# Forgetting attention: the keys' cumulative sums and the causal mask enter the logits by matmuls in PSUM instead of by VectorE

## The chip, the cores and the metric

One of the eight cores of a Trainium2 chip runs the whole kernel. The metric is device time in microseconds, the median of repeated runs. The engines are TensorE (PE, with its weight loads PEld), VectorE (DVE), ScalarE (ACT), GpSimd (POOL) and the DMA queue that SyncE (SP) issues. Everything is float32 in and out; products of full accuracy are made of three TensorE passes over a high and a low half (`hi*hi`, `hi*lo`, `lo*hi`), each half in the rounded type fp32r.

## The reference, cut to what matters

The layer normalises x (512 tokens, width 1024), projects it by one wide matrix, runs four mixers side by side (a chunked spatial gate, a top-k attention, a gated convolution, a forgetting attention), gates and merges them, and projects back. Only the forgetting attention changes:

```python
cum = jnp.cumsum(jax.nn.log_sigmoid((f_logit + b_f).astype(jnp.float32)), axis=1)
cum_k = jnp.transpose(cum, (0, 2, 1))
...
logits = jnp.einsum('bqhd,bshd->bhqs', qb, kh).astype(jnp.float32) * (FOX_HEAD_DIM ** -0.5)
logits = logits + jnp.transpose(cq, (0, 2, 1))[..., None] - cum_k[:, :, None, :]
logits = jnp.where((key_pos[None, :] <= pos_q[:, None])[None, None], logits, -jnp.inf)
p = jax.nn.softmax(logits, axis=-1).astype(vh.dtype)
o = jnp.einsum('bhqs,bshd->bqhd', p, vh)
```

So each logit gets the query's cumulative sum (one number per row and head), minus the key's cumulative sum (one number per column and head), and a mask above the diagonal.

## The kernel before, in words

Weights stream in by 256 columns (`load_w`), ScalarE and VectorE or GpSimd split them into halves (`split`, `unit`), and `proj_fm` makes a 128-feature by 512-token product of 24 matmuls of 512 columns (L119, L120, L124). Between such products the kernel calls `point()`, which advances two generators by one step: `topk_steps` (first `cumulate`, then `scores_topk`) and `attn_steps` (`attention`). A scheduler that simulates the engines then orders the instructions of each engine, so a step's work can land some matmuls earlier or later than it is written.

`scores_topk` is VectorE's longest job: for three blocks of queries it forms scores (matmuls `dots`, L458 and L459, the second with only 64 rows), and then takes 16 rounds of MAX8 and MATCH_REPLACE8 over each block (`sc1`, `sc2`, `sc3`).

`attention` runs 16 jobs, one per head h and query block i, each over n = 128(i+1) keys; `fox` is the forgetting attention. A job makes three logit matmuls into a PSUM bank `lg` (`mm3`, L88 to L90; two at i = 0, L502 and L505). Then VectorE adds the query's sum `cq` and a tile `nb[h]` of the keys' sums (L509), adds the mask to the diagonal block (L511; at i = 0 also the second half of the bank, L515), and takes the row maximum (L517). ScalarE exponentiates with the maximum as bias (L519), VectorE inverts the sum (L521), ScalarE scales (L522). Three jobs later (`lag`) TensorE transposes the result (`pt_ps`, L533), which is split into halves again, and after four jobs of a head `values` makes the products `po` with the values. The `nb[h]` tile comes from `neg_cum` (L434): the row h of the four cumulative sums is picked and split (`rh` on ScalarE, `rl` on VectorE, L84) and two matmuls with 4 rows and 512 columns (`nb_ps`, L439 and L440) spread it over 128 partitions.

Three pools matter. `tmp` gives out 512-column SBUF tiles in turn (9 of them). PSUM has 4 banks `mm` for the projections and 4 banks `at` for everything else, `lg`, `pt_ps`, `po`, `dots` among them. SBUF-to-SBUF work of GpSimd (`wl`, L81, 2.4 us each in this stage) runs beside VectorE's.

Of the kernel before, what the change touches and what calls it, by code (L numbers as in the profile page):

```python
# [8 lines left out]
F32 = mybir.dt.float32  # L9
F32R = mybir.dt.float32r  # L10
AF = mybir.ActivationFunctionType
ALU = mybir.AluOpType
# [11 lines left out]
NH = 4  # L24
# [9 lines left out]
def hybrid_kernel(ctx: ExitStack, tc, x, norm_g, w_in, gm_ln_g, gm_ln_b, gm_w_s, gm_b_s,  # L34
# [26 lines left out]
        return big(name + "h"), big(name + "l")  # L61

    def tmp(name, dtype=F32, cols=S):
        return sb.tile([P, cols], dtype, tag="tmp", name=name, bufs=9)

    def small(name, cols=1, bufs=4):
        return sb.tile([P, cols], F32, tag=name, name=name, bufs=bufs)
# [1 line left out]
    def psum(name):  # L69
        return at.tile([P, S], F32, tag="at", name=name)  # L70
# [117 lines left out]
    def load_dv(i):  # L188
# [11 lines left out]
    load_x(2)  # L200
    load_x(3)

    ident = const.tile([P, P], F32, name="ident")
    make_identity(nc, ident)
    negh = const.tile([P, 8], F32, name="negh")
    nc.vector.memset(negh, -0.5)
    causal = const.tile([P, P], F32, name="causal")
    nc.gpsimd.memset(causal, 0.0)
    nc.gpsimd.affine_select(out=causal, in_=causal, compare_op=ALU.is_ge, fill=-BIG, base=0,
                            pattern=[[-1, P]], channel_multiplier=1)  # L210
    up = const.tile([P, S], F32R, name="up")
    upf = tmp("upf")
    nc.gpsimd.memset(upf, 1.0)
# [119 lines left out]
    for u in range(2):  # L333
        ps = proj_fm(unit(rawq, u))
        qf, qs = tmp("qf"), tmp("qs")
        nc.scalar.activation(qf, ps, AF.Copy)
        nc.sync.dma_start(qs[0:64], qf[64:128])
        nc.sync.dma_start(qs[64:128], qf[0:64])

        even, odd, low = (kq[(2 + 3 * u + i) // 4][:, (2 + 3 * u + i) % 4, :] for i in range(3))  # L340
        for dst, own, other in ((even, slice(0, 64), slice(64, 128)), (odd, slice(64, 128), slice(0, 64))):
            nc.scalar.activation(dst[own], qf[own], AF.Copy)
            nc.scalar.activation(dst[other], qs[other], AF.Copy)
            nc.vector.tensor_tensor(low[own], qf[own], dst[own].bitcast(F32), op=ALU.subtract)
        qis += [(even, low), (odd, low)]
        if u == 0:
            sp = psum("sp")
            rp = psum("rp")
            nc.tensor.transpose(rp[:, 0:13], rows, ident[0:13, 0:13])
            for t in range(NT):  # L350
                nc.tensor.transpose(sp[:, 8 * t:8 * t + 8], wf[64:72, t * P:(t + 1) * P],
                                    ident[64:72, 64:72])
            prm = const.tile([P, 45], F32, name="prm")
            nc.vector.tensor_copy(prm[:, 0:32], sp[:, 0:32])
            nc.vector.tensor_copy(prm[:, 32:45], rp[:, 0:13])
            wif = prm[:, 0:32].rearrange("p (t c) -> p t c", c=8)
            kvg = prm[:, 44:45]

            sq = tmp("sq")
            nc.scalar.activation(sq, ps_c, AF.Square)  # L360
            sqh, sql = (tmp("sq" + s, F32R) for s in "hl")
            split(sqh, sql, sq)
            ms = psum("ms")
            for t in range(NT):
                ts_ = slice(t * P, (t + 1) * P)
                nc.tensor.matmul(ms[:, 2 * t:2 * t + 2], sqh[:, ts_], up[:, P:P + 2],
                                 start=True, stop=False)
                nc.tensor.matmul(ms[:, 2 * t:2 * t + 2], sql[:, ts_], up[:, P:P + 2],
                                 start=False, stop=True)
            rc = small("rc", 2 * NT, 1)  # L370
            rsqrt(rc, ms[:, 0:2 * NT], 1.0 / P, 2 * NT)
        else:

            dg = sb.tile([P, NT, P], F32, tag="tmp", name="dg", bufs=9)
            nc.vector.tensor_tensor(dg, ident[:, None, :].to_broadcast([P, NT, P]),
                                    rc[:, 0::2, None].to_broadcast([P, NT, P]), op=ALU.mult)
            dgh, dgl = (tmp("dg" + s, F32R) for s in "hl")
            split(dgh, dgl, dg.rearrange("p t c -> p (t c)"))
            rb_ = psum("rb")
            nc.tensor.matmul(rb_, up[:, P:2 * P], dgh, start=True, stop=False)  # L380
            nc.tensor.matmul(rb_, up[:, P:2 * P], dgl, start=False, stop=True)
            cn = tmp("cn")
            nc.scalar.activation(cn, ps_c, AF.Copy)
            nc.vector.tensor_tensor(cn, rb_, cn, op=ALU.mult)
            cth = const.tile([P, S], F32R, name="cth")
            ctl = const.tile([P, S], F32R, name="ctl")
            split(cth, ctl, cn, kvg)


    def flat16(tl):  # L390
        return tl.rearrange("p t h -> p (t h)")
# [15 lines left out]
    nc.vector.tensor_tensor(z_, z_, e_, op=ALU.mult)  # L407
    nc.vector.tensor_tensor(l_, l_, z_, op=ALU.add)
    nc.vector.scalar_tensor_tensor(ls, f16, 0.0, l_, op0=ALU.min, op1=ALU.subtract)
    lsh = const.tile([P, NT, NH], F32R, name="lsh")  # L410
    lsl = const.tile([P, NT, NH], F32R, name="lsl")
    split(flat16(lsh), flat16(lsl), ls)


    cq = const.tile([P, NT, NH], F32, name="cq")
    nb = {}

    def cumulate():
        ps = psum("cum")
        for j in range(NT):  # L420
            for n, part in enumerate((lsh, lsl)):
                nc.tensor.matmul(ps[0:NH, j * P:], part[:, j, :], up[:, 0:S - j * P],
                                 start=(j == 0 and n == 0), stop=(j == NT - 1 and n == 1))
        cum = tmp("cum")[0:NH, :]
        nc.scalar.activation(cum, ps[0:NH, :], AF.Copy, scale=-1.0)
        yield
        ps = psum("cq")
        for t in range(NT):
            nc.tensor.transpose(ps[:, NH * t:NH * t + NH], cum[:, t * P:(t + 1) * P],
                                ident[0:NH, 0:NH])  # L430
        nc.scalar.activation(flat16(cq), ps[:, 0:16], AF.Copy, scale=-1.0)
        nb["rows"] = cum

    def neg_cum(h):  # L434

        rh, rl = (tmp("r" + x, F32R)[0:NH, :] for x in "hl")
        split(rh, rl, nb["rows"], ident[0:NH, h:h + 1])
        ps = psum("nb_ps")
        nc.tensor.matmul(ps, up[0:NH, P:2 * P], rh, start=True, stop=False)  # L439
        nc.tensor.matmul(ps, up[0:NH, P:2 * P], rl, start=False, stop=True)  # L440
        nb[h] = tmp("nb")
        nc.scalar.activation(nb[h], ps, AF.Copy)


    msk = {0: causal}
# [43 lines left out]
    def attention(qks, vh, vl, o, fox, lag=3):  # L489
# [3 lines left out]
        def logits(h, i):  # L493
            qh, ql = qks[h][:, 0, :], qks[h][:, 1, :]
            kh, kl = key_parts(qks[h])
            n = (i + 1) * P
            qs = slice(i * P, n)
            ps = psum("lg")
            l = tmp("l")
            if i == 0:  # L500

                nc.tensor.matmul(ps[:, 0:2 * P], qh[:, qs],  # L502
                                 qks[h][:, 2:4, :].rearrange("p a c -> p (a c)")[:, 0:2 * P],
                                 start=True, stop=False)
                nc.tensor.matmul(ps[:, 0:P], ql[:, qs], kh[:, 0, :], start=False, stop=True)  # L505
            else:
                mm3(ps[:, :n], qh[:, qs], ql[:, qs], kh[:, 0:i + 1, :], kl[:, 0:i + 1, :], True, True)
            if fox:
                nc.vector.scalar_tensor_tensor(l[:, :n], ps[:, :n], cq[:, i, h:h + 1],  # L509
                                               nb[h][:, :n], op0=ALU.add, op1=ALU.add)  # L510
                nc.vector.tensor_tensor(l[:, qs], l[:, qs], causal, op=ALU.add)  # L511
            else:
                nc.vector.tensor_tensor(l[:, :n], ps[:, :n], msk[i], op=ALU.add)
            if i == 0:
                nc.vector.tensor_tensor(l[:, :n], ps[:, P:2 * P], l[:, :n], op=ALU.add)  # L515
            nm = small("nm")
            nc.vector.tensor_reduce(nm, l[:, :n], axis=AX.X, op=ALU.max, negate=True)  # L517
            se = small("se")
            nc.scalar.activation(l[:, :n], l[:, :n], AF.Exp, bias=nm, accum_out=se)  # L519
            ri = small("ri")  # L520
            nc.vector.reciprocal(ri, se)  # L521
            nc.scalar.activation(l[:, :n], l[:, :n], AF.Copy, scale=ri)  # L522
            ls[h, i] = l
# [39 lines left out]
    def fox_qk(hp):  # L563
        rq = load_w(D_Q + hp * 256)
        rk = load_w(D_K + hp * 256)
        for s in range(2):
            h = 2 * hp + s
            neg_cum(h)
            qk = qk_tile("qk")
            ps = proj_fm(unit(rq, s))  # L570
            split(qk[:, 0, :], qk[:, 1, :], ps, scale)
# [10 lines left out]
    gps = at.tile([P, NH, P], F32, tag="at", name="gps")  # L582
    for g in range(NH):
        nc.tensor.transpose(gps[:, g, :], gw[:, g * P:(g + 1) * P], ident)
    gwt = sb.tile([P, NH, P], F32, tag="tmp", name="gwt", bufs=9)
    nc.vector.tensor_copy(gwt, gps)
    nc.gpsimd.affine_select(out=gwt, in_=gwt, compare_op=ALU.is_ge, fill=0.0, base=0,
                            pattern=[[0, NH], [1, P]], channel_multiplier=-1)
# [27 lines left out]
    def mixed(cp):  # L616
        ru = load_w(A_U + cp * 256)
        for s in range(2):
            g = 2 * cp + s
            ps = proj_fm(unit(ru, s))  # L620
            gs = slice(g * P, (g + 1) * P)
            t1 = sb.tile([P, NT, P], F32, tag="tmp", name="t1", bufs=9)
            for c2 in range(0, NT, 2):
                mx = at.tile([P, 2, 2, P], F32, tag="at", name="mx")
                for c in range(2):
# [244 lines left out]
```

## Time and profile before

| | |
|---|---|
| three runs | 710.55 us median (708.91 to 711.37) |
| the profiled execution: its own time | 711.89 us |
| its span, first to last instruction | 710.2 us |
| PE busy | 693.9 us (98%), 3139 matmuls |
| DVE busy | 364.5 us (51%), of 110 to 170 us all of it |
| ACT busy | 275.1 us (39%) |
| the forgetting attention's jobs | first logits at 127.5 us, L509 of the last job at 212.2 us |

TensorE's busy time is drawn from modelled ends: in a stream of 512-column matmuls each is shown 0.39 us long, though the next starts 0.227 us after it. What a matmul costs is therefore read from one start to the next. The profile's share of DVE is a mean: it is idle most of the second half and has no gap in the stretch of the top-k rounds.

### The profile page before, as it was taken

Reading aid. Unit: us, or ns where it says so; the run is one execution under the profiler, and the core shown is the slowest. Engines: PE = TensorE matmul, PEld = TensorE weight load, DVE = VectorE, ACT = ScalarE, POOL = GpSimd, SP = SyncE. Lnnn points to the kernel's source line nnn. Section 1 sums busy time; section 2 is a strip of 40 time slices with the busy share of each in tenths; the row PEclk is TensorE's granted clock in tenths of the full one; section 3 lists DMA queues with packets and bytes.
Section 4 is the critical chain, followed back from the end, with each engine's and each line's share of the span. In section 5 each row is a group of like instructions: output and inputs, shape, how many; then the busy total and the mean of one; then the engine's idle time right before and its main releaser. Section 6 shows DMA issues by size and latency. Waiting matters only on the chain.

```text
span 710.2 us, 8000 instructions
## 1 busy us (share of the span) xinstructions
PE 693.9 (98%) x3139; PEld 566.4 (80%) x3139; DVE 364.5 (51%) x638; ACT 275.1 (39%) x439; POOL 169.9 (24%) x110
## 2 busy tenths in 40 slices
PE   7999999988999999999999999999999999999996
PEld 4878767766888888888888888888888888888885
DVE  5825699999953664634233343323522334343454
ACT  4616354354444556433322242223322223333233
POOL 1000487341333323203000021222211132111101
PEclk9999999999999999999999999999999999999999
DMA  6715031312112111242322331322313313133233
GB/s 237 219 64 153 4 118 59 112 59 69 60 60 90 60 60 60 61 147 73 105 83 96 118 114 65 119 77 102 120 60 118 117 61 119 60 118 119 62 117 119
DMA packets 56817, 68.05 MB, mean 96 GB/s; under 512 B 3582, under 2 KB 45067, under 8 KB 56780
## 3 DMA queue, kind: packets, MB, share of 16 engines
q1 hardware_dynamic: 55900, 65.46, 28.3%
q0 software_dynamic: 304, 1.05, 0.4%
q10 hardware_dynamic: 576, 1.05, 0.4%
q8 instruction: 24, 0.39, 0.2%
q14 instruction: 13, 0.11, 0.0%
HBM read 64.80 MB, written 2.10 MB: 94 GB/s over the span
## 4 chain that ended last, share of the span: by engine, by line
PE 85%; DVE 11%; DMA 2%; issue 1%; ACT 0%; SPq 0%; POOLq 0%; POOL 0%; DVEq 0%
PE ps_fm L119 18%; PE ps_fm L120 18%; PE ps_fm L124 18%; PE pb L744 4%; PE pb L745 4%; PE pb L747 4%; DVE sc L474 3%; DVE m L473 2%; PE ps_o L144 2%; PE ps_o L146 2%; PE ps_o L145 2%; DVE sc L466 1%; PE pt_ps L533 1%; PE ps_dv L144 1%; DVE l L511 1%
## 5 line engine op out<-in xcount | busy, mean ns | idle before, releaser
L119 PE MATMUL ps_fm<-hh,wh 128*128 128x512 f32 (+1 forms) x640 | 251.3, 393 | 0.0
L120 PE MATMUL ps_fm<-hl,wh 128*128 128x512 f32 (+1 forms) x640 | 250.0, 391 | 0.0
L124 PE MATMUL ps_fm<-hh,wl 128*128 128x512 f32 (+1 forms) x640 | 162.5, 391 | 0.0
L119 PEld LDWEIGHTS ps_fm<-hh,wh 128*128 128x128 f32 (+1 forms) x640 | 120.1, 188 | 26.0 <-issue 0.9
L120 PEld LDWEIGHTS ps_fm<-hl,wh 128*128 128x128 f32 (+1 forms) x640 | 120.0, 187 | 24.9 <-issue 0.2
L124 PEld LDWEIGHTS ps_fm<-hh,wl 128*128 128x128 f32 (+1 forms) x640 | 119.0, 187 | 25.0 <-issue 0.2
L80 ACT ACTIVATE wh<-raw 128x1024 fp32r<-128x1024 f32 x78 | 82.3, 1056 | 114.1 <-PE ps_fm L120 85.0
L81 DVE TENSOR_TENSOR wl<-raw,wh 128x1024 fp32r<-128x1024 f32 x50 | 61.0, 1222 | 78.4 <-PE ps_fm L124 67.1
L81 POOL TENSOR_TENSOR wl<-raw,wh 128x1024 fp32r<-128x1024 f32 x28 | 69.1, 2474 | 111.9 <-PE ps_fm L124 49.2
L753 POOL TENSOR_TENSOR acc<-acc,sg 128x512 f32<-128x512 f32 x24 | 41.8, 1742 | 155.9 <-DVE sg L752 155.9
L744 PE MATMUL pb<-yh,wh 128*128 128x512 f32 x128 | 49.8, 389 | 0.0
L745 PE MATMUL pb<-yl,wh 128*128 128x512 f32 x128 | 49.8, 389 | 0.0
L81 DVE TENSOR_TENSOR wl<-rawb,wh 128x1024 fp32r<-128x1024 f32 x16 | 19.6, 1225 | 51.3 <-PE ps_fm L124 36.8
L80 ACT ACTIVATE wh<-rawb 128x1024 fp32r<-128x1024 f32 x16 | 16.9, 1057 | 50.6 <-PE ps_fm L120 50.6
L752 DVE TENSOR_TENSOR sg<-pb,sg 128x512 f32<-128x512 f32 x24 | 16.6, 692 | 36.3 <-PE pb L747 36.3
L747 PE MATMUL pb<-yh,wl 128*128 128x512 f32 x128 | 34.2, 389 | 0.0
L519 ACT ACTIVATE l<-l,nm 128x128 f32<-128x128 f32 (+3 forms) x32 | 17.9, 560 | 28.5 <-DVE nm L517 28.5
L771 ACT ACTIVATE sg<-ps_fm 128x512 f32<-128x512 f32 x32 | 19.2, 600 | 24.4 <-PE ps_fm L124 24.4
L747 PEld LDWEIGHTS pb<-yh,wl 128*128 128x128 f32 x128 | 24.0, 188 | 5.0
L744 PEld LDWEIGHTS pb<-yh,wh 128*128 128x128 f32 x128 | 24.0, 188 | 5.0
L745 PEld LDWEIGHTS pb<-yl,wh 128*128 128x128 f32 x128 | 24.0, 188 | 5.0
L145 PE MATMUL ps_o<-wl,mh 128*128 128x512 f32 (+1 forms) x72 | 26.2, 366 | 0.0
(242 smaller groups left out, 913.9 us busy)
## 6 DMA issues: line engine op xcount, KB each, us to landing
raw<-in_w_in_dram SPq DMA_DIRECT2D x39, 1024.0 KB, 4.9
rawb<-in_w_branch_dram SPq DMA_DIRECT2D x8, 1024.0 KB, 4.9
rawt<-in_w_out_dram SPq DMA_DIRECT2D x4, 1024.0 KB, 4.9
xt<-in_x_dram SPq DMA_DIRECT2D x4, 512.0 KB, 8.3
rawt<-in_w_in_dram SPq DMA_DIRECT2D x4, 512.0 KB, 8.4
rawt<-in_w_in_dram SPq DMA_DIRECT2D x2, 1024.0 KB, 5.7
xr<-in_x_dram SPq DMA_DIRECT2D x2, 1024.0 KB, 4.9
out_dram<-o SPq DMA_DIRECT2D x4, 256.0 KB, 2.1
```

What stands on the lines that cost most here:

```text
L80: nc.scalar.activation(hi, src, AF.Copy)
L81: eng.tensor_tensor(lo, src, hi.bitcast(F32), op=ALU.subtract)
L119: nc.tensor.matmul(ps[:m], wh[:, k, :], hh[:, k, :], start=(k == 0), stop=False)
L120: nc.tensor.matmul(ps[:m], wh[:, k, :], hl[:, k, :], start=False, stop=False)
L124: nc.tensor.matmul(ps[:m], wl[:, k, :], hh[:, k, :], start=False, stop=(k == NK - 1))
L144: nc.tensor.matmul(ps, ah, wh, start=(k == 0), stop=False)
L145: nc.tensor.matmul(ps, ah, wl, start=False, stop=False)
L474: nc.vector.match_replace(out=scs[i], in_to_replace=m8, in_values=scs[i], imm_value=TAKEN)
L744: nc.tensor.matmul(pb, bh[:, k, cs_], yh[:, k, :], start=(k == 0), stop=False)
L745: nc.tensor.matmul(pb, bh[:, k, cs_], yl[:, k, :], start=False, stop=False)
L747: nc.tensor.matmul(pb, bl[:, k, cs_], yh[:, k, :], start=False, stop=(k == NH - 1))
L753: nc.gpsimd.tensor_tensor(acc, acc, sg, op=ALU.add)
```

## The change

The keys' sums are no longer spread over partitions by `neg_cum`. `cumulate` now makes the four cumulative sums twice, in rows 0 to 3 and 32 to 35 of a 36-row tile; ScalarE rounds them to fp32r (`cums`), and VectorE leaves the rounding rest in rows 32 to 35. A 36 by 4 tile `pick` holds ones at rows h and 32+h. In each job of the forgetting attention two matmuls follow the three logit products in the same bank: the identity times the causal mask on the diagonal block (128 columns, L515 of the new file), and `pick`'s column h, spread over 128 output rows, times `cums` (36 rows, n columns, L517). VectorE takes the row maximum from PSUM, and one 1-column instruction (`nb`, L523) folds the query's sum into the bias; ScalarE exponentiates from PSUM. At i = 0 the products are three of 128 columns instead of one of 256 and one of 128. The identity and the mask are kept as fp32r, made by VectorE casts from `tmp` tiles, and `tmp` has 8 tiles instead of 9. The other attention keeps its old path.

```diff
-        return sb.tile([P, cols], dtype, tag="tmp", name=name, bufs=9)
+        return sb.tile([P, cols], dtype, tag="tmp", name=name, bufs=8)
...
-    ident = const.tile([P, P], F32, name="ident")
-    make_identity(nc, ident)
+    identf = tmp("identf", cols=P)
+    make_identity(nc, identf)
+    identr = const.tile([P, P], F32R, name="ident")
+    nc.vector.tensor_copy(identr, identf)
+    ident = identr.bitcast(F32)
+
+    pick = const.tile([36, NH], F32R, name="pick")
+    nc.vector.tensor_copy(pick, identf[0:36, 0:NH])
+    nc.vector.tensor_copy(pick[32:36, :], identf[32:36, 32:36])
...
     def cumulate():
-        ps = psum("cum")
+        l36 = tmp("l36")[:, 0:144].rearrange("p (t c) -> p t c", c=36)
...
+        cum = tmp("cum")[0:36, :]
+        nc.scalar.activation(cum, ps, AF.Copy, scale=-1.0)
+        nc.scalar.activation(cums, cum, AF.Copy)
+        nc.vector.tensor_tensor(cums[32:36, :], cum[32:36, :], cums[32:36, :].bitcast(F32),
+                                op=ALU.subtract)
...
-    def neg_cum(h):
-
-        rh, rl = (tmp("r" + x, F32R)[0:NH, :] for x in "hl")
-        split(rh, rl, nb["rows"], ident[0:NH, h:h + 1])
-        ps = psum("nb_ps")
-        nc.tensor.matmul(ps, up[0:NH, P:2 * P], rh, start=True, stop=False)
-        nc.tensor.matmul(ps, up[0:NH, P:2 * P], rl, start=False, stop=True)
-        nb[h] = tmp("nb")
-        nc.scalar.activation(nb[h], ps, AF.Copy)
...
+            if fox:
+
+                ks_ = slice(0, i + 1)
+                nc.tensor.matmul(ps[:, :n], qh[:, qs], kh[:, ks_, :], start=True, stop=False,
+                                 skip_group_check=True)
+                nc.tensor.matmul(ps[:, :n], qh[:, qs], kl[:, ks_, :], start=False, stop=False,
+                                 skip_group_check=True)
+                nc.tensor.matmul(ps[:, :n], ql[:, qs], kh[:, ks_, :], start=False, stop=False,
+                                 skip_group_check=True)
+                nc.tensor.matmul(ps[:, qs], identr, causalr, start=False, stop=False,
+                                 skip_group_check=True)
+                nc.tensor.matmul(ps[:, :n], pick[:, h:h + 1].to_broadcast([36, P]), cums[:, :n],
+                                 start=False, stop=True, skip_group_check=True)
+
+                nc.vector.tensor_reduce(nm, ps[:, :n], axis=AX.X, op=ALU.max, negate=True)
+                c = cq[:, i, h:h + 1]
+                nb = small("nb")
+                nc.vector.tensor_scalar(nb, nm, c, c, op0=ALU.subtract, op1=ALU.add)
+                src, bias = ps[:, :n], nb
...
-            if fox:
-                nc.vector.scalar_tensor_tensor(l[:, :n], ps[:, :n], cq[:, i, h:h + 1],
-                                               nb[h][:, :n], op0=ALU.add, op1=ALU.add)
-                nc.vector.tensor_tensor(l[:, qs], l[:, qs], causal, op=ALU.add)
...
-            nc.scalar.activation(l[:, :n], l[:, :n], AF.Exp, bias=nm, accum_out=se)
+            nc.scalar.activation(l[:, :n], src, AF.Exp, bias=bias, accum_out=se)
...
-            neg_cum(h)
```

Because `cumulate` has become longer, the scheduler places the first score products elsewhere. On TensorE before, the third product of the spatial gate (`ps_va_747`) is interrupted for them, with 2 of its 24 matmuls and the whole fourth product (`ps_va_814`) still to come:

```order
L144 MATMUL ps_va_747<-wh_601,hh_58 128x512
L429 MATMUL cq_655<-ident_96,cum_653 128x4 x4
L458 MATMUL dots_662<-kq_407 128x256
L459 MATMUL dots_662<-kq_407,kq_408 128x256
...
L145 MATMUL ps_va_747<-wl_602,hh_58 128x512
L146 MATMUL ps_va_747<-wh_601,hl_59 128x512
L144 MATMUL ps_va_814<-wh_587,hh_58 128x512
```

On TensorE now, they come behind all four products and behind 12 matmuls of the first query projection (`ps_fm_898`; new line numbers):

```order
L119 MATMUL ps_fm_898<-hh_58,wh_894 128x512
L120 MATMUL ps_fm_898<-hl_59,wh_894 128x512
L445 MATMUL cq_669<-ident_101,cum_665 128x4 x4
L463 MATMUL dots_676<-kq_414 128x256
L464 MATMUL dots_676<-kq_414,kq_415 128x256
L463 MATMUL dots_682<-kq_414 128x256
L464 MATMUL dots_682<-kq_414,kq_415 128x256
L463 MATMUL dots_688<-kq_414,kq_415 128x256
```

The first scores thus moved behind 2 + 24 + 12 = 38 more matmuls of 512 columns. The job itself, on VectorE: before, around the third and fourth job of the first head (`l_1163`, `l_1196`), among the top-k rounds:

```order
L509 SCALAR_TENSOR_TENSOR l_1163<-lg_1162,cq_570,nb_886 128x384
L474 MATCH_REPLACE sc1_661<-m8_1566,sc1_661 128x256
L473 MAX m8_1159<-sc3_795 128x8
L515 TENSOR_TENSOR l_1095<-lg_1094,l_1095 128x128
L474 MATCH_REPLACE sc2_728<-m8_1156,sc2_728 128x384
L511 TENSOR_TENSOR l_1163<-l_1163,causal_103 128x128
L473 MAX m8_1675<-sc1_661 128x8
L474 MATCH_REPLACE sc3_795<-m8_1159,sc3_795 128x512
L517 TENSOR_REDUCE nm_1101<-l_1095 128x1
```

Now, around the first two jobs of that head (`lg_1081`, `lg_1116`):

```order
L520 TENSOR_REDUCE nm_1083<-lg_1081 128x1
L478 MAX m8_1030<-sc2_742 128x8
L478 MAX m8_952<-sc3_809 128x8
L479 MATCH_REPLACE sc1_675<-m8_1185,sc1_675 128x256
L523 TENSOR_SCALAR nb_1090<-nm_1083,cq_573 128x1
L479 MATCH_REPLACE sc2_742<-m8_1030,sc2_742 128x384
L479 MATCH_REPLACE sc3_809<-m8_952,sc3_809 128x512
L478 MAX m8_1269<-sc1_675 128x8
L542 RECIPROCAL ri_1094<-se_1092 128x1
```

Of a job's wide VectorE instructions one is left, and two of one column (L523, L542) stand beside it, with top-k rounds between them as before.

## Rows read from the trace of the kernel before

**Rows 1.** The page: busy us, share of the span, instructions.

```profile
PE 693.9 (98%) x3139; PEld 566.4 (80%) x3139; DVE 364.5 (51%) x638; ACT 275.1 (39%) x439; POOL 169.9 (24%) x110
```

**Rows 2.** The chain of waits in order of time: start, us, what.

```profile
310.08 1.81 PE ps_fm L124 x8
```

**Rows 3.** Stages: us, busy us and count of PE, PEld, DVE, ACT, POOL; clock, DMA.

```profile
160.00:169.00 9.00, 6.07 (x25) 3.86 (x24) 9.00 (x27) 3.72 (x9) 1.31 (x1) 1.00 0.03 9
169.00:173.00 4.00, 4.00 (x18) 3.77 (x17) 4.00 (x13) 2.59 (x8) 1.07 (x1) 0.57 0.46 144
```

**Rows 4.** What PE waited for: us in total, times, longest us.

```profile
PE nb_ps L440 <- DVE rl L84: 1.5, 1, 1.5
PE po L89 <- DVE ptl L81: 1.5, 1, 1.5
PE pt_ps L533 <- DVE l L515: 0.9, 1, 0.9
PE pt_ps L533 <- ACT l L522: 0.7, 2, 0.4
PE gp L263 <- DMA g<-in_norm_g_dram: 0.3, 1, 0.3
```

**Rows 5.** PE in order of time at 147 us: start, us, what.

```profile
147.29 0.33 PE L533 MATMUL pt_ps<-ident,l 128*128 128x128 f32 x1 [0.29 <-ACT l L522]
147.55 0.50 PE L439 MATMUL nb_ps<-rh,up 4*128 4x512 f32 x1
149.54 0.50 PE L440 MATMUL nb_ps<-rl,up 4*128 4x512 f32 x1 [1.49 <-DVE rl L84]
```

**Rows 6.** PE in order of time: a 4-row matmul among 128-row ones.

```profile
109.85 0.39 PE L120 MATMUL ps_fm<-hl,wh 128*128 128x512 f32 x1
110.17 0.50 PE L439 MATMUL nb_ps<-rh,up 4*128 4x512 f32 x1
110.60 0.50 PE L119 MATMUL ps_fm<-hh,wh 128*128 128x512 f32 x1
110.94 0.39 PE L120 MATMUL ps_fm<-hl,wh 128*128 128x512 f32 x1
```

**Rows 7.** PE in order of time: a 64-row matmul among 128-row ones.

```profile
102.37 0.39 PE L458 MATMUL dots<-kq 128*128 128x512 f32 x1
102.69 0.49 PE L459 MATMUL dots<-kq 64*128 64x512 f32 x1
103.11 0.50 PE L119 MATMUL ps_fm<-hh,wh 128*128 128x512 f32 x1
103.45 0.40 PE L120 MATMUL ps_fm<-hl,wh 128*128 128x512 f32 x1
```

**Rows 8.** PE in order of time: 256-column and 128-column matmuls.

```profile
155.75 0.28 PE L90 MATMUL lg<-qk 128*128 128x256 f32 x1
155.87 0.49 PE L533 MATMUL pt_ps<-ident,l 128*128 128x128 f32 x3
156.11 0.95 PE L124 MATMUL ps_fm<-hh,wl 128*128 128x512 f32 x3
```

**Rows 9.** DVE's busy us (count) from 127.4 to 168.7 us, of L509 alone.

```profile
127.40:168.70 41.30, 3.44 (x7) 1.00 0.20 67
```

**Rows 10.** The same of L511 alone.

```profile
127.40:168.70 41.30, 7.55 (x7) 1.00 0.20 67
```

**Rows 11.** PE, PEld and DVE of tile rl alone, 80 to 168.7 us.

```profile
80.00:168.70 88.70, 1.98 (x4) 0.72 (x4) 3.09 (x4) 1.00 0.22 72
```

**Rows 12.** DVE and POOL in order of time at 135.8 us.

```profile
135.82 2.40 POOL L81 TENSOR_TENSOR wl<-raw,wh 128x1024 fp32r<-128x1024 f32 x1 [4.61 <-PE ps_fm L124]
135.89 2.47 DVE L511 TENSOR_TENSOR l<-l,causal 128x128 f32<-128x128 f32 x1
```

**Rows 13.** Lines L511 and L521: count: min/median/max ns, first and last start.

```profile
L511 DVE TENSOR_TENSOR l<-l,causal x16: 264/277/2471, 135.9 to 213.5; 128x128 f32<-128x128 f32 x16
L521 DVE RECIPROCAL ri<-se x32: 131/154/166, 146.7 to 290.6; 128x1 f32<-128x1 f32 x32
```

More of the change, by code (lines that the diff above doesn't have):

```diff
@@ L201, in hybrid_kernel @@
     load_x(3)
-    ident = const.tile([P, P], F32, name="ident")
-    make_identity(nc, ident)
+    identf = tmp("identf", cols=P)
[6 more added lines that the diff above has]
+    nc.vector.tensor_copy(pick[32:36, :], identf[32:36, 32:36])
     negh = const.tile([P, 8], F32, name="negh")
     nc.vector.memset(negh, -0.5)
-    causal = const.tile([P, P], F32, name="causal")
-    nc.gpsimd.memset(causal, 0.0)
-    nc.gpsimd.affine_select(out=causal, in_=causal, compare_op=ALU.is_ge, fill=-BIG, base=0,
+    causalf = tmp("causalf", cols=P)
+    nc.gpsimd.memset(causalf, 0.0)
+    nc.gpsimd.affine_select(out=causalf, in_=causalf, compare_op=ALU.is_ge, fill=-BIG, base=0,
                             pattern=[[-1, P]], channel_multiplier=1)
+    causalr = const.tile([P, P], F32R, name="causal")
+    nc.vector.tensor_copy(causalr, causalf)
+    causal = causalr.bitcast(F32)
     up = const.tile([P, S], F32R, name="up")
@@ L372, in hybrid_kernel @@
         else:
-            dg = sb.tile([P, NT, P], F32, tag="tmp", name="dg", bufs=9)
+            dg = sb.tile([P, NT, P], F32, tag="tmp", name="dg", bufs=8)
             nc.vector.tensor_tensor(dg, ident[:, None, :].to_broadcast([P, NT, P]),
@@ L409, in hybrid_kernel @@
     nc.vector.scalar_tensor_tensor(ls, f16, 0.0, l_, op0=ALU.min, op1=ALU.subtract)
-    lsh = const.tile([P, NT, NH], F32R, name="lsh")
-    lsl = const.tile([P, NT, NH], F32R, name="lsl")
-    split(flat16(lsh), flat16(lsl), ls)
     cq = const.tile([P, NT, NH], F32, name="cq")
-    nb = {}
+    cums = const.tile([36, S], F32R, name="cums")
     def cumulate():
-        ps = psum("cum")
+        l36 = tmp("l36")[:, 0:144].rearrange("p (t c) -> p t c", c=36)
+        nc.vector.memset(l36, 0.0)
+        for c0 in (0, 32):
+            nc.vector.tensor_copy(l36[:, :, c0:c0 + NH], ls.rearrange("p (t h) -> p t h", h=NH))
+        parts = [tmp("ls" + x, F32R)[:, 0:144].rearrange("p (t c) -> p t c", c=36) for x in "hl"]
+        split(parts[0], parts[1], l36)
+        ps = psum("cum")[0:36, :]
         for j in range(NT):
-            for n, part in enumerate((lsh, lsl)):
-                nc.tensor.matmul(ps[0:NH, j * P:], part[:, j, :], up[:, 0:S - j * P],
+            for n, part in enumerate(parts):
+                nc.tensor.matmul(ps[:, j * P:], part[:, j, :], up[:, 0:S - j * P],
                                  start=(j == 0 and n == 0), stop=(j == NT - 1 and n == 1))
-        cum = tmp("cum")[0:NH, :]
-        nc.scalar.activation(cum, ps[0:NH, :], AF.Copy, scale=-1.0)
+        cum = tmp("cum")[0:36, :]
[3 more added lines that the diff above has]
+                                op=ALU.subtract)
         yield
@@ L428, in cumulate @@
         for t in range(NT):
-            nc.tensor.transpose(ps[:, NH * t:NH * t + NH], cum[:, t * P:(t + 1) * P],
+            nc.tensor.transpose(ps[:, NH * t:NH * t + NH], cum[0:NH, t * P:(t + 1) * P],
                                 ident[0:NH, 0:NH])
         nc.scalar.activation(flat16(cq), ps[:, 0:16], AF.Copy, scale=-1.0)
-        nb["rows"] = cum
-    def neg_cum(h):
-        rh, rl = (tmp("r" + x, F32R)[0:NH, :] for x in "hl")
-        split(rh, rl, nb["rows"], ident[0:NH, h:h + 1])
-        ps = psum("nb_ps")
-        nc.tensor.matmul(ps, up[0:NH, P:2 * P], rh, start=True, stop=False)
-        nc.tensor.matmul(ps, up[0:NH, P:2 * P], rl, start=False, stop=True)
-        nb[h] = tmp("nb")
-        nc.scalar.activation(nb[h], ps, AF.Copy)
     msk = {0: causal}
@@ L499, in logits @@
             l = tmp("l")
[L500 to L505, printed above, removed]
-            else:
-                mm3(ps[:, :n], qh[:, qs], ql[:, qs], kh[:, 0:i + 1, :], kl[:, 0:i + 1, :], True, True)
-            if fox:
-                nc.vector.scalar_tensor_tensor(l[:, :n], ps[:, :n], cq[:, i, h:h + 1],
-                                               nb[h][:, :n], op0=ALU.add, op1=ALU.add)
-                nc.vector.tensor_tensor(l[:, qs], l[:, qs], causal, op=ALU.add)
-            else:
+            nm = small("nm")
@@ new lines, in logits @@
+            if fox:
[15 more added lines that the diff above has]
+                src, bias = ps[:, :n], nb
+            else:
+                if i == 0:
+                    nc.tensor.matmul(ps[:, 0:2 * P], qh[:, qs],
+                                     qks[h][:, 2:4, :].rearrange("p a c -> p (a c)")[:, 0:2 * P],
+                                     start=True, stop=False)
+                    nc.tensor.matmul(ps[:, 0:P], ql[:, qs], kh[:, 0, :], start=False, stop=True)
+                else:
+                    mm3(ps[:, :n], qh[:, qs], ql[:, qs], kh[:, 0:i + 1, :], kl[:, 0:i + 1, :], True, True)
@@ L513, in logits @@
                 nc.vector.tensor_tensor(l[:, :n], ps[:, :n], msk[i], op=ALU.add)
[L514 to L517, printed above, removed]
+                if i == 0:
+                    nc.vector.tensor_tensor(l[:, :n], ps[:, P:2 * P], l[:, :n], op=ALU.add)
+                nc.vector.tensor_reduce(nm, l[:, :n], axis=AX.X, op=ALU.max, negate=True)
@@ L518, in logits @@
+                src, bias = l[:, :n], nm
             se = small("se")
-            nc.scalar.activation(l[:, :n], l[:, :n], AF.Exp, bias=nm, accum_out=se)
+            nc.scalar.activation(l[:, :n], src, AF.Exp, bias=bias, accum_out=se)
             ri = small("ri")
@@ L584, in hybrid_kernel @@
         nc.tensor.transpose(gps[:, g, :], gw[:, g * P:(g + 1) * P], ident)
-    gwt = sb.tile([P, NH, P], F32, tag="tmp", name="gwt", bufs=9)
+    gwt = sb.tile([P, NH, P], F32, tag="tmp", name="gwt", bufs=8)
     nc.vector.tensor_copy(gwt, gps)
@@ L621, in mixed @@
             gs = slice(g * P, (g + 1) * P)
-            t1 = sb.tile([P, NT, P], F32, tag="tmp", name="t1", bufs=9)
+            t1 = sb.tile([P, NT, P], F32, tag="tmp", name="t1", bufs=8)
             for c2 in range(0, NT, 2):
```

## The prediction

> **What bounds the kernel now.** I read the page first: TensorE is busy 98% of the span, VectorE 51% [rows 1]. The chain in order of time says where TensorE alone sets the pace: from about 176 us on it is a string of matmuls, eight of 512 columns in 1.81 us, so 0.227 us each [rows 2]. There, work added to TensorE is added to the time, and nothing that VectorE saves is seen. Before 169 us it is different. The table by stage shows VectorE without a gap (9.00 of 9.00 us) while TensorE is busy 6.07 of 9.00, and then four microseconds at a granted clock of 0.57, a mixture of the two levels of 2.4 and 1.2 GHz, right behind TensorE's longest idle stretch [rows 3]. The list of waits says what TensorE stood for: VectorE's `rl` 1.5 us, `ptl` 1.5, `l` 0.9, ScalarE's `l` 0.7, five waits, 4.6 us [rows 4]. The view draws matmuls longer than they take: from 147.55 to 149.54 us are 1.99 us, the matmul's own share is 0.227, so 1.76 were lost where 1.49 are shown [rows 5]. Five times 0.27 more makes 6.0 us lost, and the slow clock 0.43 of 4 us, 1.7 us. That is all that a faster VectorE can give back: 7.7 us.
>
> **What the change adds to TensorE.** A matmul of fewer than 128 rows between full ones costs more than its columns. Around a 4-row one the starts lie 0.32, 0.43 and 0.34 us apart, 1.09 together, where without it two steps of 0.227 would stand: 0.64 us for one instruction, 0.41 of it beyond its columns [rows 6]. Around a 64-row one it is 0.32, 0.42 and 0.34, so 0.63 and 0.40 [rows 7]. The `pick` matmul has 36 rows, between the two, and I take 0.40. To this come its columns: 0.227 for 512, 0.12 for 256, 0.08 for 128 [rows 2, 8], 0.18 for 384 (between 256 and 512). A head has one of each: 4 x 0.40 + 0.61 = 2.21 us, four heads 8.8 us (7.8 to 9.6, as a short neighbour hides part of the switch or is itself slowed by it).
>
> The mask's matmul has 128 columns. Three such take 0.24 us, 0.08 each [rows 8]; one right ahead of a 4-row matmul took 0.26 to the next start, of which the switch's first part is 0.09 (0.32 less 0.227), leaving 0.17 [rows 5, 6]. It stands in just that place, but with its weights loadable ahead: I take 0.12, for 16 jobs 1.9 us (1.3 to 2.7). At i = 0 three products of 128 columns replace one of 256 and one of 128: 0.24 to 0.36 us for 0.20, four times, 0.4 us (0.2 to 0.6). Added together: 11.1 us (9.3 to 12.9).
>
> Row and rule differ about the first of these. The rows show that a matmul of few rows delays itself and the next two. The Trainium skill (TensorE: Matmul & The Clock Gate, section Step-by-step: what each phase is for) says that the next weights load while the present matmul runs, and that the row count does not matter for it. By that rule `pick` would cost its columns alone, 2.4 us instead of 8.8. The 12 `dots` and 8 `nb_ps` matmuls of this trace disagree.
>
> **What it takes away from TensorE.** Eight `nb_ps` matmuls at 0.64 us: 5.1 us. Both ends are the same row, so the term is firm.
>
> **What it does for the waits.** Up to 168.7 us VectorE loses 3.4 us of L509, 7.6 of L511 and 3.1 of `rl` [rows 9 to 11], 14.1 us. L511 takes 0.28 us by its median, so seven should take 1.9; one at 135.89 took 2.47 and ended just behind GpSimd's 2.40 us of `wl` [rows 12, 13], and the 7.6 hold some two more of that kind. Against this stand seven or eight new one-column instructions, 0.15 us each by L521, the nearest of that size [rows 13], 1.2 us; the row maximum stays, only from PSUM. Net relief: 12.9 us. But the top-k work starts later: the order puts 38 more 512-column matmuls ahead of the first scores, 38 x 0.227 = 8.6 us. So at the products with the values, where VectorE was latest, it is 12.9 - 8.6 = 4.3 us better off than before, more than the 1.76 us by which it was late. At the first transposes (147 us before) only three of the four `rl`, four L509 and two or three L511 have been saved, some 7 to 9 us, about what the later start takes; there VectorE is as tight as it was. I therefore leave 1.0 us of the 6.0 standing (0 to 6.0), and with the idle stretch at 167 us gone I count the slow clock as gone too, 1.7 us (0 to 1.7).
>
> What is late next is TensorE itself. Behind the row maximum, in VectorE's order, stand two or three top-k rounds before `nb`, and ScalarE's exponential waits for that; behind ScalarE's wait stand the weight splits (`wh`). Job and transposes lie some 50 matmuls apart, over 11 us, which covers this.
>
> **What I cost at nothing.** The casts of identity and mask at the start: TensorE stands 0.3 us for the DMA of the norm's weights right behind the warm-up [rows 4], which hides a cast of 128 columns; without that cover it would be 0.1 to 0.3 us. The wider `cumulate` (a memset, two small copies, one more ScalarE pass): it runs beside the spatial gate's last product, of 24 matmuls. ScalarE's four `rh` and `nb` passes go, its exponential only changes its source: it is busy 39% [rows 1]. One `tmp` tile fewer: the four long-lived `nb` tiles and the four times two halves are gone as well, so the attention needs fewer; in the later gating stages TensorE runs without a gap and few tiles are alive. VectorE's savings behind 169 us: nothing waits for them.
>
> **The sum.** +11.1 - 5.1 - 5.0 - 1.7 = -0.7 us. Made against the profiled execution (711.89 us, span 710.2) this gives 711.2; that execution was 1.3 us above the median of the three runs, and against the median it is 709.9. A run of this kernel can tell about 0.3%, 2.1 us, from no change, so the forecast is no change: 0.60, with its own range from 9.3 - 5.1 - 6.0 - 1.7 = -3.5 to 11.9 - 5.1 - 3.0 - 0.9 = +2.9, that is 707.1 to 713.5.
>
> **The rivals.**
>
> The waits stay: slower. The place is the top-k rounds between 130 and 169 us. If the 8.6 us later start weighs as much as the relief, for instance because the score instructions now meet GpSimd's `wl` work, which could hold VectorE's two-input instructions as it held L511 [rows 12], VectorE reaches the first jobs late and TensorE stands as long as before. Then only the matmuls count: +11.1 - 5.1 = +6.0, 716.6 us. It decides from a net relief at or below nothing, 8.6 us against what is saved by then. For it speaks that VectorE had no gap at all in this stage [rows 3]; against it that at the worst wait the balance is 4.3 us to the good. Chance 0.18.
>
> `pick` does not switch the array: faster. If 36 rows run like 128, the 16 times 0.40 us go: -0.7 - 6.4 = -7.1, 702.8 us. That is also what the rule above from the Trainium skill (TensorE: Matmul & The Clock Gate) gives. For it speaks only that no row here has 36 rows; against it the rows with 4 and with 64, which agree within 0.01 us [rows 6, 7]. Chance 0.10.
>
> The logits' bank is held longer: slower. Before, L509 frees the bank for most jobs; now the exponential on ScalarE does, behind maximum, two or three top-k instructions and `nb`. With four `at` banks for logits, transposes, products and `dots`, TensorE could wait for a bank. No wait of TensorE for a bank is in the list now [rows 4]. By an estimate, a wait as long as the shortest in that list, 0.3 us, in each of 16 jobs would be 4.8 us; with the rest as forecast 714.7. It decides when a bank is held longer than TensorE takes to come round its four banks. Chance 0.12.
>
> **Chances.** Of the forecast's 0.60, 0.11 lie below -2.1 us and 0.10 above +2.1. Faster: 0.11 + 0.10 = 0.21. Slower: 0.10 + 0.18 + 0.10 of the third rival = 0.38, of which I move 0.05 to no change, as a part of the waits should go even there: 0.33. Same: 0.46. The range leaves out half of the second rival and half of the first: 706.0 to 716.0.
>
> **What would show it.** In the new profile: 16 `pick` matmuls whose next three starts lie about 0.40 us further apart than columns alone; no `nb_ps`; matmuls in the first stages at the same spacing; waits of TensorE between 130 and 170 us that sum to about 1 us, and no stage at a clock below 1.00 at 170 us; L511 and L509 gone, GpSimd's `wl` no longer met by wide two-input instructions in the job. From about 180 us the new kernel should fall behind the old one step by step by 16 jobs' price for those jobs still to come. The forecast is wrong if waits of TensorE on VectorE or on ScalarE's `l` sum to over 3 us, or if the switch costs under 0.2 us.

## The result

| | us | ratio to the kernel before, 95% interval |
|---|---|---|
| before, four runs | 710.72 (708.91 to 711.37) | |
| after, four runs | 722.34 (721.92 to 722.88) | 1.0165 [1.0142, 1.0188] |
| after, the profiled execution | 721.92, span 720.0 | |

The changed kernel is 11.6 us slower. The prediction said 709.9 us, no change, with a range of 706.0 to 716.0.

The page of the changed kernel: busy us, share of the span and instructions, and from its part on the chain, the shares by engine.

```profile
PE 707.6 (98%) x3167; PEld 568.4 (79%) x3167; DVE 349.8 (49%) x622; ACT 272.2 (38%) x432; POOL 167.5 (23%) x110
...
PE 96%; DMA 2%; issue 1%; DVE 0%; ACT 0%; SPq 0%; POOLq 0%; POOL 0%
```

VectorE and ScalarE have less to do than before [rows 1] and are off the path; the chain is TensorE alone. The waits are in order too. What TensorE waited for in the changed kernel (us in total, times, longest), the whole list:

```profile
PE pt L247 <- DVE xs L238: 3.6, 2, 2.4
PE warm L268 <- DVE ident L206: 2.3, 1, 2.3
PE ps_dv L145 <- DVE dvwl L81: 0.3, 1, 0.3
```

All three are at the start. Each of the five waits between 130 and 169 us that the prediction counted [rows 4] is gone. The same stretch by stage (us, busy us and count of PE, PEld, DVE, ACT and POOL, granted clock, DMA):

```profile
160.00:170.00 10.00, 10.00 (x52) 8.21 (x51) 9.28 (x30) 4.08 (x10) 4.25 (x2) 1.00 0.01 2
170.00:180.00 10.00, 10.00 (x52) 8.20 (x51) 9.06 (x26) 3.74 (x9) 2.96 (x2) 1.00 0.33 105
```

No idle TensorE and no slow clock, where before there were 6.07 of 9.00 us busy and a clock of 0.57 [rows 3]. So the time is not lost where the change was made. It is lost in matmuls that the change doesn't touch. The chain of waits (start, us, what) at the place of [rows 2]:

```profile
321.99 1.87 PE ps_fm L124 x8
```

Eight 512-column matmuls that took 1.81 us take 1.87, 0.234 us each instead of 0.227. The table by stage shows it some 190 us behind the last job of the forgetting attention, where both kernels only project and merge. First the kernel before, then the changed one:

```profile
400.00:440.00 40.00, 40.00 (x178) 33.14 (x177) 14.62 (x17) 13.33 (x18) 8.15 (x5) 1.00 0.32 105
```

```profile
400.00:440.00 40.00, 40.00 (x173) 32.27 (x172) 15.40 (x17) 13.36 (x17) 7.68 (x5) 1.00 0.29 94
```

The clock is full in both, TensorE has no gap, and yet 173 matmuls fall in 40 us instead of 178. Averaged over all steps of under 240 ns from one full 512-column matmul to the next in the two traces, the spacing is 227.3 ns before (2577 steps) and 232.4 ns after (2551). That is 5.1 ns in each, 13.1 us in all, more than the whole slowdown. It is there long before the attention: from 20 to 40 us such steps take 227.9 ns before and 234.1 after.

### The profile page after: what moved, and what is told of

Same layout as the page of the kernel before. It is cut to its first block, busy times and chain, and to the rows that moved or that the text cites. A ratio compares the mean times of both kernels' runs of the same rounds, so it can differ in the third digit from the quotient of the medians.

```text
span 720.0 us, 8031 instructions
## 1 busy us (share of the span) xinstructions
PE 707.6 (98%) x3167; PEld 568.4 (79%) x3167; DVE 349.8 (49%) x622; ACT 272.2 (38%) x432; POOL 167.5 (23%) x110
## 4 chain that ended last, share of the span: by engine, by line
PE 96%; DMA 2%; issue 1%; DVE 0%; ACT 0%; SPq 0%; POOLq 0%; POOL 0%
PE ps_fm L119 21%; PE ps_fm L124 21%; PE ps_fm L120 21%; PE pb L764 4%; PE pb L765 4%; PE pb L767 4%; PE ps_o L144 2%; PE ps_o L145 2%; PE ps_o L146 2%; PE pt_ps L554 1%; PE ps_va L145 1%; PE ps_va L146 1%; PE ps_va L144 1%; PE ps_dv L145 1%; PE ps_dv L146 1%; PE ps_dv L144 1%
## 5 line engine op out<-in xcount | busy, mean ns | idle before, releaser
L119 PE MATMUL ps_fm<-hh,wh 128*128 128x512 f32 (+1 forms) x640 | 254.8, 398 | 0.0
L120 PE MATMUL ps_fm<-hl,wh 128*128 128x512 f32 (+1 forms) x640 | 253.4, 396 | 0.0
L124 PE MATMUL ps_fm<-hh,wl 128*128 128x512 f32 (+1 forms) x640 | 167.2, 398 | 0.0
L144 PE MATMUL ps_o<-wh,mh 128*128 128x512 f32 (+1 forms) x72 | 26.1, 365 | 0.0
```

What stands on the lines that cost most here:

```text
L119: nc.tensor.matmul(ps[:m], wh[:, k, :], hh[:, k, :], start=(k == 0), stop=False)
L120: nc.tensor.matmul(ps[:m], wh[:, k, :], hl[:, k, :], start=False, stop=False)
L124: nc.tensor.matmul(ps[:m], wl[:, k, :], hh[:, k, :], start=False, stop=(k == NK - 1))
L144: nc.tensor.matmul(ps, ah, wh, start=(k == 0), stop=False)
```

## The experiments

What can reach matmuls that run before the first new instruction of the attention, and 190 us behind the last? Two things the change does to the whole program. It moves tiles: `pick` and `cums` are new and `lsh` and `lsl` are gone, so all that is allocated behind them, the weights `wh` and `wl` and the working tiles among it, lies 1952 bytes further in each partition, while `hh` and `hl`, which are allocated first, stay. Or the new instructions leave something behind. The start addresses below are those of the built programs.

### Tiles moved by 32 bytes

After, with a wider tile (E1), and before, with a wider tile (E2):

```diff
-    pick = const.tile([36, NH], F32R, name="pick")
+    pick = const.tile([36, 12], F32R, name="pick")[:, 0:NH]
```

```diff
-    negh = const.tile([P, 8], F32, name="negh")
+    negh = const.tile([P, 16], F32, name="negh")
```

E1: 

> The changed kernel with the tile `pick` made 32 bytes wider, and nothing else: every tile allocated behind it then starts at the same remainder modulo 64 bytes as in the kernel before (the weights' and the working tiles at 0 instead of 32). Theory A, the addresses: the 512-column matmuls return from 231 to 238 ns apart to 227 ns, and with some 2550 of them 5.2 ns each, 13 us, come back: 709 us (707.5 to 711.5). Rival B, something that the new instructions do (36 rows, a stationary broadcast from one column, matmuls between fp32r tiles), or the ring of temporary tiles cut from nine to eight: the pace stays at 231 to 238 ns and the time at 722 us.

E2: 

> The kernel before with the tile `negh` made 32 bytes wider, and nothing else: the weights' and the working tiles start at 32 modulo 64 bytes, as in the changed kernel, with not one instruction of the change. Theory A: the pace becomes 231 to 238 ns and the time 710.7 + 13 = 724 us (720 to 726). Rival B: 227 ns and 710.7 us.

In E3 and E4 a 32-byte tile also stands ahead of the working tiles, with and without the wider `pick`:

```diff
+    gap = sb.tile([P, 8], F32, tag="gap", name="gap", bufs=1)
+    nc.vector.memset(gap, 0.0)
     xts = [pt_tile("xt", F32, (P, 2, D)) for _ in range(2)]
```

E3: 

> The changed kernel with the weights' pool back at 0 modulo 64 bytes (`pick` 32 bytes wider) and the pool of working tiles still at 32 (a 32-byte tile, filled once, ahead of it). If the place of the weights sets the pace (A1): 227 ns and 709 us. If that of the working tiles does (A2, which for the projections would be the vector and scalar engines' traffic beside them, since their operands hh and hl haven't moved): 231 to 238 ns and 722 us. Both in part: between. Rival B: 722 us.

E4: 

> The changed kernel with the weights' pool left at 32 modulo 64 bytes and the pool of working tiles back at 0 (the same 32-byte tile ahead of it, `pick` as it was). A1, the weights: pace 231 to 238 ns, 722 us. A2, the working tiles: 227 ns and 709 us. Rival B: 722 us.

Measured, against 710.85 us for before on the same chip: E1 714.7 us, 1.0056 [1.0037, 1.0075]; E2 718.25, 1.0105 [1.0085, 1.0126]; E3 716.0, 1.0080 [1.0056, 1.0105]; E4 724.23, 1.0191 [1.0170, 1.0212]. The chain of E1, then of E2:

```profile
407.56 1.83 PE ps_fm L124 x8
```

```profile
413.12 1.87 PE ps_fm L124 x8
```

E2 settles the main point: not one instruction of the change is in it, and it has the changed kernel's pace and 7.4 of its 11.6 us. The rival, new instructions or the shorter ring of `tmp`, can't explain that. But neither number came out in size. E1 went only two thirds of the way, so "0 modulo 64 bytes" is not what the weights want. And E3 and E4, with working tiles moved too, each lost 1.3 to 1.9 us more, whichever way they were moved. A row shows where. The products of the merge, `yh` (a working tile) times `wl`, four matmuls in the chain, in the changed kernel and in E3:

```profile
381.60 0.91 PE pb L767 x4
```

```profile
397.33 0.93 PE pb L769 x4
```

In the changed kernel weights and working tiles are moved together, and this product runs at 0.227 us each (0.91 us in all 28 such rows); in E3 they were moved by different amounts, and it takes 0.233. That suggested that the place of neither operand matters by itself, but their distance. (In E1, moved together too, 4 such rows have 0.91 and 23 have 0.92, of which more below.)

(E2's loss is smaller than its pace alone would make it, 1809 slow steps x 6.0 ns = 10.9 us. TensorE's waits at the attention shrank to the following two rows of its list, and its clock stayed at 1.00 where before it was 0.57 [rows 3, 4]; that the slower stream gave VectorE the time for this is likely, but not shown.)

```profile
PE po L89 <- DVE ptl L81: 1.2, 1, 1.2
PE pt_ps L533 <- ACT l L522: 0.7, 1, 0.7
```

### The distance between the two operands

E5 is the changed kernel with `pick` 28 columns wide; its instructions stand in the same order on every engine. E6 is before with `negh` 40 columns wide. (E5, E6 and the later E8 and E11 also keep one statistics tile in 3 buffers instead of 4, for room.) From here on "A2" in the expectations is the distance, not the working tiles. E7 is before with everything moved, `hh` and `hl` too:

```diff
-    hh = act.tile([P, NK, S], F32R, name="hh")
+    hh = act.tile([P, 8 + NK * S], F32R, name="hh")[:, 8:].rearrange("p (k s) -> p k s", s=S)
```

E5: 

> The changed kernel, every instruction in the same order, with `pick` padded so that the weights' and the working tiles start at the same remainder modulo 512 bytes as hh and hl (128), as they do in the kernel before. Theory A2, what counts is the distance between the start of the moving and that of the stationary operand (weights less hh, modulo 128 bytes: 0 in the kernel before at 227 ns, 64 at 229.8 ns in the run shifted by 32 bytes, 32 at 232.4 ns in the changed kernel): 227 ns throughout, and 714.7 - 2580 x 2.5 ns = 708.2 us (707 to 710), which is what the prediction's sum of -0.7 us gives. Rival: the rest of the slowdown is the new instructions' own: 229.8 ns and 714.7 us.

E6: 

> The kernel before with everything from the causal mask on 128 bytes further (`negh` wider by 128 bytes), so that the weights lie 128 bytes, modulo 512, from hh and hl. If the distance counts modulo 128 bytes or less: 227 ns and 710.8 us. If it counts over a longer stretch: above 227 ns, at 229.8 ns 717.4 us.

E7: 

> The kernel before with 32 bytes ahead of hh, so that hh, hl, the weights and the working tiles all start at 32 modulo 128 bytes, at distance 0 from each other. If the distance between the operands counts (A2): 227 ns and 710.8 us. If the place of each operand by itself counts (A1, an operand not on a multiple of 64 or 128 bytes is read more slowly): 232 ns or more and 718 us or more, as with the run of the kernel before in which the weights alone were at 32.

Measured, against 710.18 us for before: E5 708.39, 0.9984 [0.9973, 0.9996]; E6 717.73, 1.0106 [1.0086, 1.0127]; E7 709.89, 0.9992 [0.9977, 1.0008]. The chain of E5, of E6 and of E7:

```profile
405.27 1.81 PE ps_fm L124 x8
```

```profile
407.02 1.87 PE ps_fm L124 x8
```

```profile
406.09 1.81 PE ps_fm L124 x8
```

E7 has every operand at 32 modulo 128 and runs at the full pace, so places alone don't count. Its weights and working tiles have the same addresses as in E2; only `hh`, `hl` and two small constant tiles lie 32 bytes further, and the loss is gone. E5 has the whole change and nothing of the loss: 14.0 us lie between it and the changed kernel (12.9 by the two ratios), by the place of the tiles alone. E6 says that 128 bytes are not a full turn.

E9 and E10 put several distances into one program. They are the kernel before with eight `tmp` tiles, and `wl` alone spaced out, so that its four buffers lie at four distances from `hh` (E9 with 32 bytes; E10 with 128). In E9 a tile of 384 bytes ahead of the working tiles keeps these at distance 0 from `wh`. The edit of E10:

```diff
-        return tuple(wpool.tile(shape, F32R, tag="w" + s, name="w" + s, bufs=4) for s in "hl")
+        wh = wpool.tile(shape, F32R, tag="wh", name="wh", bufs=4)
+        wl = wpool.tile([P, 32 + shape[1] * shape[2]], F32R, tag="wl", name="wl", bufs=4)
+        return wh, wl[:, 32:].rearrange("p (a c) -> p a c", c=shape[2])
```

E9: 

> The kernel before (with eight temporary tiles, to make room) with its four buffers of wl, the low half of the weights, at distances of 32, 64, 96 and 128 bytes (modulo 512) from hh; wh, hl and all else stay at distance 0. If the distance between moving and stationary operand of a matmul counts: the pairs hh, wh and hl, wh stay at 227 ns, and the eight matmuls hh, wl of a projection run at some 232, 230, 232 and 231 ns by turns of four, as the whole kernels at distances 32, 64, 96 and 128 did; about a third of 2580 matmuls x 4.5 ns = 3.9 us on 710.7: 714 to 715 us. If the slower pace is a state of the whole kernel (a code or a buffer placed otherwise), all three pairs slow down alike.

E10: 

> The same with the four buffers of wl at distances 128, 256, 384 and 0 modulo 512 bytes. The distance theory says 231 ns at 128 and 227 ns at 0. For 256 and 384: 227 ns if the pattern repeats at 256 bytes (then 384 is like 128, 231 ns); 229 ns or more at both if it repeats at 512 or later. 711.5 to 713.5 us.

The chain of E10, four projections in a row; by the addresses their `wl` lies 256, 0, 384 and 128 bytes (modulo 512) from `hh`:

```profile
406.38 1.81 PE ps_fm L126 x8
411.82 1.81 PE ps_fm L126 x8
417.26 1.86 PE ps_fm L126 x8
422.76 1.86 PE ps_fm L126 x8
```

256 is like 0 and 384 like 128: the pattern repeats at 256 bytes. In the same two programs the pairs with `wh`, still at distance 0, keep 227.4 ns (E10) and 228.5 ns (E9, slowed next to `wl`), so the whole kernel is not in one slower state. E9's four distances, 64, 128, 96 and 32, are all slow (the 230 ns expected for 64 came from E1, whose distance is 192):

```profile
404.11 1.86 PE ps_fm L126 x8
409.63 1.86 PE ps_fm L126 x8
415.12 1.87 PE ps_fm L126 x8
420.65 1.86 PE ps_fm L126 x8
```

The mean step from a matmul to the next, by distance of its stationary from its moving operand modulo 256 bytes: 0, 227.3 to 227.4 ns (before, E5, E7, and E10 from 0 to 0); 32, 233.3 (E2); 64, 233.7 (E9); 96, 233.9 (E9); 128, 232.7 (E6); 160, 233.6 (the changed kernel); 192, 229.6 (E1); 224, 232.9 (E3, the merge). Groups of over 100 steps at the same distance agree within 1 ns from run to run, but for distance 0: where a program holds slow pairs as well, its pairs at 0 have 227.5 (E10), 227.7 (E6), 228.0 (E2), 228.5 (E9), 228.7 (the changed kernel) and 229.3 ns (E1). The merge shows where that comes from. In E2 the first five steps of its 28 merges, right behind a projection at distance 32, take 228.6 to 235.5 ns by their means, and from the sixth on 226.5 to 227.0; in E7, with `yh` and `wh` at the same addresses as in E2, all have 226.5 to 227.0. In the changed kernel it is the first eight steps, in E1 the first ten. So the slower pace runs on for some matmuls into pairs at distance 0. Why it does is not shown.

As times E9 and E10 missed: both 717.4 us, 1.0074 [1.0054, 1.0094] of 712.07. The pace of `wl` in E10 makes only 377 steps x 5.6 ns = 2.1 us. Most of the rest lies at the attention. In E10 TensorE waits there in the following row (4.5 us in E9, against 4.8 in all in the kernel before), and its clock is 0.77 from 160 to 170 us and 0.71 from 170 to 180, against 0.97 and 0.86 before:

```profile
PE pt_ps L535 <- ACT l L524: 7.6, 2, 7.2
```

These two programs have the old VectorE path and eight `tmp` tiles instead of nine, and the attention stalls at 160 us; the changed kernel has eight and doesn't. That would fit the view that it needs fewer, but no run took the ninth tile away and nothing else, so it is not shown.

### The matmuls of pick

E8 is E5 with `pick` and `cums` filled up with zeros to 128 rows; E11 is E5 without the 16 `pick` matmuls (the keys' sums are left out).

```diff
-    pick = const.tile([36, 28], F32R, name="pick")[:, 0:NH]
-    nc.vector.tensor_copy(pick, identf[0:36, 0:NH])
+    pick = const.tile([P, 28], F32R, name="pick")[:, 0:NH]
+    nc.vector.tensor_copy(pick, identf[:, 0:NH])
...
-    cums = const.tile([36, S], F32R, name="cums")
+    cums = const.tile([P, S], F32R, name="cums")
+    zeros = tmp("zeros")
+    nc.gpsimd.memset(zeros, 0.0)
+    nc.gpsimd.tensor_copy(cums, zeros)
...
-                nc.tensor.matmul(ps[:, :n], pick[:, h:h + 1].to_broadcast([36, P]), cums[:, :n],
+                nc.tensor.matmul(ps[:, :n], pick[:, h:h + 1].to_broadcast([P, P]), cums[:, :n],
```

E8: 

> The changed kernel at distance 0, with `pick` and `cums` filled up with zeros to 128 rows, so that the 16 matmuls that add the key sums have 128 rows like their neighbours. If the 0.39 us around each 36-row matmul (0.43 us to the next start, then 0.34, less two spacings of 0.227, and 0.08 us ahead) is the price of the row count: 16 x 0.39 = 6.2 us less than the run at distance 0 with 36 rows, 702 us (700.5 to 704.5). If that time belongs to the stationary's broadcast from one column, or to the group with the mask: 708.2 us.

E11: 

> The changed kernel at distance 0 without the 16 matmuls of pick; the keys' cumulative sums are left out of the logits by this. The prediction's term for pick was 8.8 us (16 x 0.40 for the switch of rows, and the columns): 708.4 - 8.8 = 699.6 us (698.5 to 701). The run with 128 rows says that 5.3 us of it is the row count; the rest, 3.5 us, must be the columns (16 x 320 x 0.44 ns = 2.3 us) and what lies around them. If the waits for the top-k and the soft-max come back when TensorE has less to do (rival): 703 us or more.

E8 took 703.11 us, 0.9904 [0.9889, 0.9920], 5.3 us less than E5 on the same chip. In order of time on TensorE, a `pick` of 36 rows in E5, then the one of 128 rows at the same place in E8:

```profile
126.33 0.22 PE L515 MATMUL lg<-causal,ident 128*128 128x128 f32 x1
126.48 0.38 PE L517 MATMUL lg<-cums,pick 36*128 36x256 f32 x1
126.79 0.50 PE L119 MATMUL ps_fm<-hh,wh 128*128 128x512 f32 x1
127.13 0.40 PE L120 MATMUL ps_fm<-hl,wh 128*128 128x512 f32 x1
127.36 0.39 PE L119 MATMUL ps_fm<-hh,wh 128*128 128x512 f32 x1
```

```profile
125.06 0.22 PE L518 MATMUL lg<-causal,ident 128*128 128x128 f32 x1
125.13 0.33 PE L520 MATMUL lg<-cums,pick 128*128 128x256 f32 x1
125.30 0.40 PE L119 MATMUL ps_fm<-hh,wh 128*128 128x512 f32 x1
125.54 0.40 PE L120 MATMUL ps_fm<-hl,wh 128*128 128x512 f32 x1
125.77 0.39 PE L119 MATMUL ps_fm<-hh,wh 128*128 128x512 f32 x1
```

From the mask to the third full matmul behind it are 1.03 us with 36 rows and 0.71 with 128, at 256 columns both times: 0.32 us, and 16 of these make 5.1. With `pick` at full rows its step is 0.17 us, 0.05 longer than the 0.12 of 256 columns [rows 8]. In E11, with no `pick`, the same 0.05 stands in the step behind the mask's, 0.28 us for 512 columns instead of 0.23, so it is the mask's, and the broadcast from one column costs nothing that shows:

```profile
125.63 0.22 PE L515 MATMUL lg<-causal,ident 128*128 128x128 f32 x1
125.69 0.44 PE L119 MATMUL ps_fm<-hh,wh 128*128 128x512 f32 x1
125.97 0.40 PE L120 MATMUL ps_fm<-hl,wh 128*128 128x512 f32 x1
```

E11 took 701.26 us, 0.9852 [0.9835, 0.9868]: against E5 that is 7.1 us by the medians and 9.4 by the ratios (E11 ran on another chip, where before ran at 712.07); it lies just above the 698.5 to 701 expected. TensorE had no wait in the attention there either, so the rival falls. E8, the change with both costs taken out, is the fastest full version.

## Why the prediction was wrong

**The step that failed** is the one the first paragraph starts from: "from about 176 us on it is a string of matmuls, eight of 512 columns in 1.81 us, so 0.227 us each". I read that as the price of such a matmul and kept it for every matmul that the change doesn't touch. It is the price at distance 0 between the operands, and the change moved the weights from distance 0 to 160 (modulo 256). "What I cost at nothing" names the casts, the wider `cumulate`, one `tmp` tile fewer, and not that two new tiles and two dropped ones move all others. Of the signs listed, "matmuls in the first stages at the same spacing" is the one that came out wrong, and it was wrong from the first projection on. The two things that the prediction named as showing it wrong, waits of over 3 us and a switch under 0.2 us, did not come; neither looks at matmuls that the change leaves alone. The size of the missed term is shown by one edit: E5 gives back 12.9 to 14.0 us, where the spacing accounts for 13.1.

**The sum itself** held: E5, which has the same instructions, is 0.9984 of before [0.9973, 0.9996], 1.1 us faster (0.3 to 1.9), where the sum said 0.7. That is closer than its terms were known: `pick` is measured within some 2 us, the 5.1 us of `nb_ps` not by itself at all, and 1 us of waits that was left standing went, so part of the agreement may be luck.

- `pick`, 8.8 us (7.8 to 9.6): 7.1 to 9.4 by leaving it out. The switch of rows was put at 16 x 0.40 = 6.4 and measured 5.3, 0.33 each. The prediction weighed a rule of the Trainium skill (TensorE: Matmul & The Clock Gate, section Step-by-step: what each phase is for) by which it would cost nothing. E5 against E8 contradicts that and bears out the rows with 4 and 64 rows [rows 6, 7]. The rival that `pick` does not switch the array is refuted. (Its time was added up wrong: 709.9 less 6.4 is 703.5; the 702.8 takes off the 0.7 twice.)
- The waits: 1.0 us was left standing, 0 to 6.0; none stood, and the slow clock went with them, as forecast. E5 shows it without the help of a slower TensorE: it has no wait in the attention and a clock of 1.00 as well. So "the waits stay" is refuted for this kernel, and "the bank is held longer" too, since no wait on a bank is in the list of the changed kernel or of E5.
- The mask: 0.12 us each was taken. Ahead of a 36-row `pick` the next start comes 0.15 us later, with the first part of the switch in it; ahead of a 128-row one of 256 columns or more 0.06, with 0.05 more in the step behind, 0.11 together.
- The forecast's own range: its upper end takes 11.9 us for the matmuls where the terms add up to 12.9, so it should be 714.5 instead of 713.5. This bears on nothing here.

**What stays open.** Why distance 192 costs some 2 ns and the others about 6 wasn't tried. Nor is it shown whether the weights that are loaded during a matmul or those it uses are at odds with its moving operand: in E10 both the step into a pair at 128 (232.4 ns, 29 steps) and the step out of it (233.2, 28) are slow. One thing speaks for the loaded ones. From the merge's `yh`, `wl` at distance 0 into a pair `hh`, `wh` at 32 (E2), 128 (E6), 160 (the changed kernel) or 192 (E1) the step takes 226.6 to 226.7 ns (27 steps in each): there the weights that are loaded lie at 0 from the operand that streams at the time. The slow step out doesn't fit that, unless it is the pace that runs on.

## What to carry to other kernels

A pace read from a trace belongs to the addresses of that build: when a change adds or drops a tile, see what moves behind it, and compare the spacing of untouched matmuls before explaining anything else. In a kernel bound by TensorE with fp32r matmuls like these, allocate moving and stationary tiles at a distance of a multiple of 256 bytes, which here was worth 13 to 14 us of 722. A matmul of few rows among full ones is cheaper when filled up with zero rows (5.3 us for 16 of them).

## What the runs showed of the hardware

The distance between the start addresses of the two operands in a partition sets the pace of a 128-row, 512-column fp32r stream: 227 ns at 0 or 256 bytes, 229 to 234 at all seven other multiples of 32 bytes up to 224, with the granted clock at 1.00 and no wait in the profile. Behind a slow stretch up to ten matmuls at distance 0 are slow as well (E1). The Trainium skill (SBUF — State Buffer, section A bandwidth-pool intuition that's wrong (but worth ruling out)) gives the weight load a second, independent read port beside that of the moving operand. By that the distance would change nothing; E2, E5, E7 and E10 say that it does, by up to 6 ns of 227. A matmul of 36 rows among ones of 128 costs 0.33 us beyond its columns (E5 against E8).
